# RWKV scan of a two-layer backbone: operands without zero halves, and a state tile apart from the values

## The chip, the cores and the metric

The kernel runs on one core of one Trainium2 chip. The metric is the device time of one execution in microseconds (us); several executions are timed, and one is profiled. The engines are named as the profile names them: PE is TensorE's matmul, PEld its weight load, DVE is VectorE, ACT is ScalarE, POOL is GpSimd, SP is SyncE, which issues the DMA transfers.

## The reference, cut to what matters

A backbone of two layers runs over 1024 latent and 256 context tokens. Each layer projects its input once for four groups of heads (mLSTM, Hyena, retention, RWKV-7), runs the groups, and mixes their outputs through one output projection; a feed-forward network follows. The RWKV group has four heads of 64 channels. For each head and direction it keeps a 64 x 64 state S and does for every token, in short:

```
S <- S diag(w_t) + (S a_t) b_t^T + v_t k_t^T
y_t = S r_t
```

The kernel does this in chunks of 64 tokens: within a chunk it forms the products of a, r with b, k (the tiles G), inverts a unit lower triangular 64 x 64 matrix for each head (the tile XT), and then updates the state once per chunk. All products are float32.

## The kernel before, in words

Each layer runs projections and retention first, and then the stretch of the scan: the generator `rwkv` for ten stages, woven into `mlstm` and `ada_steps` (the side work), and at last `load_wo` and the output projection. Stage s handles one tile of 128 tokens forward and one backward (index d), two chunks each (index c or ch), two feature halves (f) and in each an even and an odd head (q). Within iteration s the program is written in the order inverse of stage s+1, chain of stage s, tail of stage s+1, prep of stage s+2; the order of instructions on each engine is then set by the framework's scheduler from its own timing model, so that an edit at one place can move rows at others.

- `rwkv_prep` loads r, k, a (rkk), V into VSA and again into SV, multiplies W2 by TWA (L492, PSUM tile pbank), and makes AR (a and r scaled by decays; L524 and L525) and bk (b and k; L515, L526). AR has two halves of columns for each head parity, and in each the other parity's 64 rows are zero: they are cleared once, ahead of the scan (L450). The products bk x AR (L529) go to the PSUM tile dbank, and a masked copy of them is G (L530). Corners of G go to NB (L535, L536); bk is transposed through dbank (L540) into bt (L541).
- `rwkv_inverse` transposes NB into LM (L550) and runs 31 steps of two operations on POOL for one half and on DVE for the other (L557, L558): the longest string of small operations in a stage.
- `rwkv_tail` builds XT.
- `rwkv_chain` is the recurrence over chunks, twice per stage (i) and per direction. In one PSUM tile (cbank) it sums b0 = G x V + AR x state (L611, L612), copies it to U (L614), multiplies by XT (L615), copies the result to VSA (L617), sums b2 = identity x state + bt x VSA (L621, L622), and scales b2 into the next state in SV (L624). y is summed in ybank (L629, L630) and added into YF (L637). V stands in SV beside the state, in the other 64 rows, because L611 and L612 share a 128-row operand there.

PSUM tiles come from pools: cbank 2, ybank 1, pbank 1, dbank 2, mbank 2 (mbank is the side work's).

Of the kernel before, what the change touches and what calls it, by code (L numbers as in the profile page):

```python
# [10 lines left out]
F32=mybir.dt.float32  # L11
F32R=mybir.dt.float32r
BF16=mybir.dt.bfloat16
ACTF=mybir.ActivationFunctionType
# [415 lines left out]
def rwkv(K,l,pv,last,p1,p2,p3):  # L430
# [8 lines left out]
    TWA=p1.tile([128,2,2,128],F32,name="TWA"); nc.gpsimd.memset(TWA,0.0)  # L439
# [4 lines left out]
    for a in range(2):  # L444
        r=slice(64,128) if a==0 else slice(0,64); o=slice(0,64) if a==0 else slice(64,128)
# [3 lines left out]
    AR=[p1.tile([128,2,2,2,2,2,64],F32,name="AR%d"%i) for i in range(3)]  # L449
    for t in AR: nc.gpsimd.memset(t[64:128,:,:,:,0],0.0); nc.gpsimd.memset(t[0:64,:,:,:,1],0.0)  # L450
    XT=[p1.tile([128,2,4,128],F32,name="XT%d"%i) for i in range(2)]
# [18 lines left out]
def rwkv_prep(K,C,s):  # L470
# [3 lines left out]
    VSA,SV=[p.tile([128,2,2,2,2,64],F32,tag=n,name=n,bufs=2) for n in ("VSA","SV")]  # L474
    f,g=FWT[s],BWT[s]
    ALL=slice(0,2); PAIR=[(ALL,slice(f,g+1,g-f))] if f<g else [(0,f),(1,g)]
    for i in range(2):
        r=slice(i*64,i*64+64); tw=K.D['twa'][r].rearrange("p (n t) -> p n t",t=128)
        for o,n in PAIR: nc.sync.dma_start(C['TWA'][r,i,o],tw[:,n])
    for o,n in PAIR: nc.sync.dma_start(rkk[:,o],K.D['wrk'][:,n])  # L480
    for q in range(2):
        r=slice(64,128) if q==0 else slice(0,64)
        for X in (VSA,SV):
            for o,n in PAIR: nc.sync.dma_start(X[r,q,o].rearrange("p d c f e -> p d (c f e)") if o is ALL else X[r,q,o].rearrange("p c f e -> p (c f e)"),K.D['wv'][n,q].rearrange("n p c x -> p n (c x)") if o is ALL else K.D['wv'][n,q].rearrange("p c x -> p (c x)"))
    VSA,SV=[X.rearrange("p q d c f e -> p d c q f e") for X in (VSA,SV)]
# [27 lines left out]
    for a in range(2):  # L513
        for ft in range(2): act(out=bk[:,:,ft,:,a],in_=As[:,:,ft].rearrange("p d (c t) -> p d c t",t=64),func=ACTF.Identity,scale=C['kas'][:,a,0,ft:ft+1],bias=C['kas'][:,a,1,ft:ft+1])
        for d in range(2): tt(out=bk[:,d,:,:,a],in0=bk[:,d,:,:,a],in1=v4(rkk[:,d,4-2*a:6-2*a]),op=A.mult)  # L515
# [930 lines left out]
```

## Time and profile before

| | |
|---|---|
| time of three runs | median 4255.34 us (4251.47 to 4255.76) |
| profiled execution | 4269.9 us, its span 4268.0 us |
| mean granted TensorE clock | 0.94 of full |
| busy share of the span | PE 93%, PEld 75%, DVE 63%, ACT 33%, POOL 23% |
| scan of layer 0, first inverse's start to last one's end | about 806 to 1159 us |
| scan of layer 1 | about 2987 to 3353 us |

The shares are means over stages with different limits: most of the span is projections and feed-forward network, where PE streams without a break; the two scans are 719 us of 4268 together. In the rows below, "PE MATMUL" rows count each float32 product twice, since it runs as two passes. Behind the bar of a row of groups stands its busy time in us and the mean duration of one instruction in ns.

### The profile page before, as it was taken

The numbers are of one execution on the slowest core, as the hardware profiler recorded it, in microseconds if no ns is written. First come the engines' busy times: TensorE is split into PE (matmuls) and PEld (weight loads), VectorE is DVE, ScalarE is ACT, GpSimd is POOL, SyncE is SP. The second block draws the span as 40 slices with busy tenths as digits, with TensorE's granted clock in tenths as the row PEclk, the third lists the DMA queues.
The fourth block names the chain that finished last, engine by engine and source line by source line (L and its number), as shares of the span: only waits on it lengthen the run. The fifth ranks groups of instructions, "written<-read, shape, count | busy, mean of one in ns | idle before, by whom it ended". The sixth has DMA issues, their size and how long they took to land.

```text
span 4268.0 us, 65334 instructions
## 1 busy us (share of the span) xinstructions
PE 3956.8 (93%) x24976; PEld 3210.9 (75%) x24976; DVE 2672.2 (63%) x5412; ACT 1416.9 (33%) x2855; POOL 979.7 (23%) x2158
## 2 busy tenths in 40 slices
PE   5999999699979999999997999996899899999998
PEld 3878877566668888888884688885666678888886
DVE  5655665789769444444449555676888684444447
ACT  4433343554344211211123433344544342112121
POOL 3320023466512000000021221024666320000002
PEclk6999999789989999999998999997899699999999
DMA  4235444343343111111113235553332431111112
GB/s 166 74 102 177 149 153 122 112 143 116 122 160 119 45 40 34 41 40 35 37 35 124 82 91 154 169 162 114 122 115 84 136 114 55 48 41 55 45 50 99
DMA packets 477138, 414.16 MB, mean 97 GB/s; under 512 B 48827, under 2 KB 443284, under 8 KB 474010
## 3 DMA queue, kind: packets, MB, share of 16 engines
q1 hardware_dynamic: 476826, 409.99, 31.0%
q8 instruction: 197, 3.23, 0.3%
q14 instruction: 115, 0.94, 0.1%
HBM read 323.65 MB, written 86.25 MB: 96 GB/s over the span
## 4 chain that ended last, share of the span: by engine, by line
PE 52%; DVE 11%; DMA 3%; issue 2%; POOL 1%; ACT 1%; SPq 0%; ACTq 0%; DVEq 0%; POOLq 0%
PE bank L1022 9%; PE bank L1023 9%; PE bank L1024 9%; PE dbank L1022 6%; PE dbank L1023 6%; PE dbank L1024 6%; DVE bst L983 1%; DMA xt<-x 1%; DVE facc L1205 1%; PE bank L186 1%; PE bank L187 1%; DMA wst<-in_w_out 1%; PE dbank L529 0%; DVE facc L1206 0%; DVE facc L1274 0%
## 5 line engine op out<-in xcount | busy, mean ns | idle before, releaser
L1022 PE MATMUL dbank<-uh,wh 128*128 128x512 f32 (+1 forms) x2120 | 765.3, 370 | 8.8 <-ACT tmpB L398 5.7
L1023 PE MATMUL dbank<-ul,wh 128*128 128x512 f32 (+1 forms) x2120 | 761.2, 368 | 0.0
L1016 DVE TENSOR_TENSOR wl<-wst,wh 128x1024 fp32r<-128x1024 f32 x146 | 185.5, 1272 | 491.9 <-ACT wh L1015 367.3
L1024 PE MATMUL dbank<-uh,wl 128*128 128x512 f32 (+1 forms) x2120 | 480.6, 367 | 0.0
L1022 PEld LDWEIGHTS dbank<-uh,wh 128*128 128x128 f32 x2120 | 401.4, 189 | 85.0 <-ACT tmpB L398 6.1
L1023 PEld LDWEIGHTS dbank<-ul,wh 128*128 128x128 f32 x2120 | 401.6, 189 | 68.9 <-issue 1.1
L1024 PEld LDWEIGHTS dbank<-uh,wl 128*128 128x128 f32 x2120 | 365.9, 188 | 70.5 <-issue 1.5
L1264 DVE TENSOR_TENSOR facc<-facc,bank 128x512 f32<-128x512 f32 x324 | 221.8, 686 | 205.1 <-PE bank L1024 205.1
L1022 PE MATMUL bank<-uh,wh 128*128 128x512 f32 (+1 forms) x920 | 334.9, 372 | 4.5 <-ACT uh L1010 4.5
L1233 POOL MEMSET fz<- 128x1 f32 x132 | 7.2, 98 | 1433.6 <-DVE fc L1248 1433.6
L1023 PE MATMUL bank<-ul,wh 128*128 128x512 f32 (+1 forms) x920 | 335.1, 372 | 0.8 <-DVE ul L1011 0.8
L1022 PE MATMUL bank<-wdh,gh 128*128 128x512 f32 x792 | 314.9, 400 | 17.9 <-DVE facc L1278 8.7
L1023 PE MATMUL bank<-wdl,gh 128*128 128x512 f32 x792 | 310.5, 392 | 1.0 <-DVE wdl L1016 1.0
L1024 PE MATMUL bank<-wdh,gl 128*128 128x512 f32 x792 | 248.1, 392 | 0.0
L1015 ACT ACTIVATE wh<-wst 128x1024 fp32r<-128x1024 f32 x146 | 154.8, 1060 | 238.1 <-PE dbank L1023 168.4
L1015 ACT ACTIVATE wdh<-wst 128x1024 fp32r<-128x1024 f32 x46 | 48.8, 1062 | 529.4 <-PE bank L1024 427.7
L558 POOL TENSOR_TENSOR XL<-XL,lt 128x48 f32<-128x48 f32 (+26 forms) x620 | 204.4, 330 | 47.7
L557 POOL TENSOR_TENSOR lt<-LM,XL 128x48 f32<-128x48 f32 (+26 forms) x620 | 187.1, 302 | 119.4 <-ACT XL L551 45.0
L1024 PE MATMUL bank<-uh,wl 128*128 128x512 f32 (+1 forms) x920 | 211.9, 372 | 0.0
L1022 PEld LDWEIGHTS bank<-uh,wh 128*128 128x128 f32 x920 | 174.1, 190 | 36.1 <-ACT uh L1010 5.6
L1023 PEld LDWEIGHTS bank<-ul,wh 128*128 128x128 f32 x920 | 174.2, 189 | 31.9 <-DVE ul L1011 1.7
L1022 PEld LDWEIGHTS bank<-wdh,gh 128*128 128x128 f32 x792 | 149.7, 189 | 59.4 <-DVE facc L1278 14.9
(476 smaller groups left out, 8132.3 us busy)
## 6 DMA issues: line engine op xcount, KB each, us to landing
wst<-in_ffn_w_up SPq DMA_DIRECT2D x88, 512.0 KB
adaw<-in_ada_w SPq DMA_DIRECT2D x160, 256.0 KB
wst<-in_w_in SPq DMA_DIRECT2D x58, 512.0 KB
wst<-in_ffn_w_down SPq DMA_DIRECT2D x46, 512.0 KB
df<-in_c_F SPq DMA_DIRECT2D x10, 1344.0 KB
xt<-x SPq DMA_DIRECT2D x26, 512.0 KB
df<-in_c_I SPq DMA_DIRECT2D x8, 1344.0 KB
rkk<-wrk SPq DMA_DIRECT2D x10, 1024.0 KB
```

What stands on the lines that cost most here:

```text
L186: mm(dst_re,F[:,i],pre(slot),start=True,stop=False); mm(dst_re,F[:,i+1],pim(slot),start=False,stop=True)
L187: mm(dst_im,F[:,i],qim(slot),start=True,stop=False); mm(dst_im,F[:,i+2],qre(slot),start=False,stop=True)
L557: e.tensor_tensor(out=t_,in0=LM[:,j,j+1:32].unsqueeze(2).to_broadcast([128,n,m]),in1=X[h][:,j:j+1,0:m].to_broadcast([128,n,m]),op=A.mult)
L558: e.tensor_tensor(out=X[h][:,j+1:32,0:m],in0=X[h][:,j+1:32,0:m],in1=t_,op=A.add)
L983: for h in range(2): nc.vector.bn_stats(out=st[:,h],in_=x[h])
L1015: k.nc.scalar.activation(out=h,in_=st,func=ACTF.Copy)
L1016: k.nc.vector.tensor_tensor(out=lo,in0=st,in1=h,op=ALU.subtract)
L1022: mm(ps,lh,rh,start=(i==0),stop=False)
L1023: mm(ps,lh,rl,start=False,stop=False)
L1024: for i,((lh,ll),(rh,rl)) in enumerate(pairs): mm(ps,ll,rh,start=False,stop=(i==n-1 and more is None))
L1205: for o,i,gg in zip([y[:,h] for h in hs],x,[g[:,h] for h in hs]) if parts else [(y,x,g)]: stt(out=o,in0=i,scalar=m,in1=gg,op0=ALU.subtract ...
L1264: else: tt(out=d,in0=d,in1=ps,op=ALU.add)
```

## The change

AR loses its zero half: 64 columns of even heads stand in rows 0 to 63, those of odd heads in rows 64 to 127, and each DVE or POOL operation that fills it now covers 128 rows at once, so that one takes the place of two. TWA and XT are halved in the same way, and the memsets of AR and TWA go. Products that had 128 rows with a zero half become two products of 64 rows, one in each half of the array's rows: G has sixteen per stage in place of eight, those of a direction in two banks, one for each parity q, and the W2 products stand in the same way. pbank is gone: the W2 products take both dbanks, and ybank has two banks, one for each parity. SV, the second copy of V, is replaced by S, which holds the state alone; its load of V (two or four transfers in a stage's prep, 60 in all) goes, b2's identity product is one of 128 x 128 in place of four, and the next state is written by one DVE operation in place of two. In b0 and b1 all products are now 64 x 64; y has 128 x 64 products of G and 64 x 64 ones of AR.

```
-    AR=[p1.tile([128,2,2,2,2,2,64],F32,name="AR%d"%i) for i in range(3)]
-    for t in AR: nc.gpsimd.memset(t[64:128,:,:,:,0],0.0); nc.gpsimd.memset(t[0:64,:,:,:,1],0.0)
+    AR=[p1.tile([128,2,2,2,2,64],F32,name="AR%d"%i) for i in range(3)]
...
-    VSA,SV=[p.tile([128,2,2,2,2,64],F32,tag=n,name=n,bufs=2) for n in ("VSA","SV")]
+    VSA=p.tile([128,2,2,2,2,64],F32,tag="VSA",name="VSA",bufs=2)
+    S=p.tile([128,2,2,2,64],F32,tag="SV",name="S",bufs=2)
...
-    bb=[K.pbank(),K.pbank()]
-    for i in range(2):
-        for d in range(2):
-            for ft in range(2):
-                o=slice(d*256+ft*128,d*256+ft*128+128); mm(bb[i][:,o],C['W2'][:,o],C['TWA'][:,i,d],start=True,stop=True)
+    bb=[bank(),bank()]
+    for d in range(2):
+        for ft in range(2):
+            for i in range(2):
+                r=slice(i*64,i*64+64); o=slice(d*256+ft*128,d*256+ft*128+128); mm(bb[i][:,o],C['W2'][r,o],C['TWA'][r,d],start=True,stop=True)
...
-        for q in range(2):
-            r=slice(q*64,q*64+64)
-            (nc.gpsimd if d==0 else nc.vector).tensor_tensor(out=ar[r,d,:,:,q,0],in0=v4(rkk[r,d,6:8]),in1=Wp[r],op=A.mult)
-            tt(out=ar[r,d,:,:,q,1],in0=v4(rkk[r,d,0:2]),in1=W[r],op=A.mult)
+        (nc.gpsimd if d==0 else nc.vector).tensor_tensor(out=ar[:,d,:,:,0],in0=v4(rkk[:,d,6:8]),in1=Wp,op=A.mult)
+        tt(out=ar[:,d,:,:,1],in0=v4(rkk[:,d,0:2]),in1=W,op=A.mult)
...
-        for c in range(2):
-            b=bank()
-            for f in range(2): mm(b[:,f*256:f*256+256],bk[:,d,f,c].rearrange("p a t -> p (a t)"),ar[:,d,f,c].rearrange("p q a t -> p (q a t)"),start=True,stop=True)
+        b=[bank(),bank()]
+        for cf in range(4):
+            for q in range(2):
+                r=slice(q*64,q*64+64); c,f=cf//2,cf%2
+                mm(b[q][:,cf*128:cf*128+128],bk[r,d,f,c].rearrange("p a t -> p (a t)"),ar[r,d,f,c].rearrange("p a t -> p (a t)"),start=True,stop=True)
...
-                for r,q in HQ: mm(b0[r,f*64:f*64+64],G[64-q*64:128-q*64,d,ch,f,q,0:64],SV[64-q*64:128-q*64,d,ch,q,f],start=True,stop=False)
-                for r,q in HQ: mm(b0[r,f*64:f*64+64],ar[:,d,f,ch,q,0],SV[:,d,ch,q,f],start=False,stop=True)
+                for q in range(2): mm(b0[H[1-q],f*64:f*64+64],G[H[q],d,ch,f,q,0:64],VSA[H[q],d,ch,q,f],start=True,stop=False)
+                for q in range(2): mm(b0[H[1-q],f*64:f*64+64],ar[H[q],d,f,ch,0],S[H[q],d,ch,f],start=False,stop=True)
...
-                for f in range(2):
-                    for r,q in HQ: mm(b2[r,f*64:f*64+64],K.ident[:,r],SV[:,d,ch,q,f],start=True,stop=False)
-                    for r,q in HQ: mm(b2[r,f*64:f*64+64],bt[:,d,ch,f,q],VSA[:,d,ch,q,f],start=False,stop=True)
-                bv=b2.rearrange("p (f e) -> p f e",f=2); SN,cn=(SV,1-ch) if i==0 else (Pn['SV'],d)
-                for r,q in HQ: tt(out=SN[r,d,cn,q],in0=bv[r],in1=rho[r,i,d].unsqueeze(2).to_broadcast([64,2,64]),op=A.mult)
+                mm(b2,K.ident,S[:,d,ch].rearrange("p f e -> p (f e)"),start=True,stop=False)
+                for f in range(2):
+                    for q in range(2): mm(b2[H[q],f*64:f*64+64],bt[:,d,ch,f,q],VSA[:,d,ch,q,f],start=False,stop=f==1)
+                SN,cn=(S,1-ch) if i==0 else (Pn['S'],d)
+                tt(out=SN[:,d,cn],in0=b2.rearrange("p (f e) -> p f e",f=2),in1=rho[:,i,d].unsqueeze(2).to_broadcast([128,2,64]),op=A.mult)
...
-                    for d in range(2): mm(yo(q,d,f),ar[:,d,f,i^d,q,1],SV[:,d,i^d,q,f],start=False,stop=True)
+                for d in range(2):
+                    for q in range(2): mm(yo(q,d,f),ar[H[q],d,f,i^d,1],S[H[q],d,i^d,f],start=False,stop=True)
...
-        psum(k,cbank=2,ybank=1,pbank=1,dbank=2,mbank=2)
+        psum(k,cbank=2,ybank=2,dbank=2,mbank=2)
```

The scheduler makes its order anew, and two places on PE show what comes of it. The first is the prep of the first stages in layer 0, where PE works through the G products (L529), the transposes of bk (L540) and the next stage's W2 products (L492). Before, in PE's order:

```order
L529 MATMUL dbank_6817<-AR0_6743,bk_6799 128x256 x2
L529 MATMUL dbank_6821<-AR0_6743,bk_6799 128x256 x2
L492 MATMUL pbank_7034<-TWA_6727,W2_6721 128x128 x4
L540 MATMUL dbank_6829<-ident_72,bk_6799 128x128 x4
L529 MATMUL dbank_6841<-AR0_6743,bk_6799 128x256 x2
L492 MATMUL pbank_7436<-TWA_6727,W2_6721 128x128 x4
L529 MATMUL dbank_6845<-AR0_6743,bk_6799 128x256 x2
L540 MATMUL dbank_6853<-ident_72,bk_6799 128x128 x4
```

After, at the same place, where the lines have become L528 (G products), L539 (transposes) and L491 (W2 products); L711 and L717 are the mLSTM's. The first two rows are the last of four such pairs:

```order
L528 MATMUL dbank_6803<-AR0_6739,bk_6787 128x128
L528 MATMUL dbank_6804<-AR0_6739,bk_6787 128x128
L539 MATMUL dbank_6819<-ident_72,bk_6787 128x128 x4
L528 MATMUL dbank_6829<-AR0_6739,bk_6787 128x128 x4
L528 MATMUL dbank_6830<-AR0_6739,bk_6787 128x128 x4
L711 MATMUL mbank_7626<-me_7617,cmdec_7528 128x10 x4
L539 MATMUL dbank_6845<-ident_72,bk_6787 128x128 x4
L717 MATMUL mbank_7633<-cmsel_7529,mW_7612 128x12 x7
L491 MATMUL dbank_7021<-TWA_6724,W2_6718 128x128 x4
```

Two things moved. The G products of the forward direction alternate between two banks, that is between the two halves of the array's rows, while those of the backward direction come four and four, each four in one half. And the W2 products of the next stage, which stood between the G products and had a bank of their own, stand behind the last transpose.

The second place is the chain of a stage in the middle of layer 0's scan. Before, PE has the products of y (L629, L630) among those of b2 (L621, L622), and all four use 128 rows and 64 columns of the array:

```order
L621 MATMUL cbank_9438<-SV_7015,ident_72 64x64 x2
L622 MATMUL cbank_9438<-VSA_7014,bt_7073 64x64 x2
L629 MATMUL ybank_9346<-VSA_7014,G_7072 64x64
L630 MATMUL ybank_9346<-SV_7015,AR1_6744 64x64 x2
L629 MATMUL ybank_9346<-VSA_7014,G_7072 64x64 x2
L733 MATMUL mbank_8012<-ident_72,mk_8013 128x128 x2
```

After, the same products are L619 (identity, 128 x 128), L621 (bt), L628 (G, 128 x 64) and L630 (AR, 64 x 64); L739 and L973 are side work:

```order
L619 MATMUL cbank_9356<-S_7007,ident_72 128x128
L621 MATMUL cbank_9356<-VSA_7006,bt_7061 64x64 x4
L628 MATMUL ybank_9331<-VSA_7006,G_7060 64x64
L628 MATMUL ybank_9332<-VSA_7006,G_7060 64x64
L739 MATMUL mbank_7852<-mV_7526,kb_7847 64x65 x4
L973 MATMUL mbank_7859<-adaw_7817,sc_83 2x128 x4
L973 MATMUL mbank_7859<-adaw_7819,sc_83 2x128 x4
L630 MATMUL ybank_9331<-S_7007,AR1_6740 64x64
L630 MATMUL ybank_9332<-S_7007,AR1_6740 64x64
```

The shape of the array's use now changes between L619 and L621 and between L628 and L630, and no longer between the two lines of b0, which are both 64 x 64. Over the whole scan such changes between neighbours on PE, counted in the two orders, go from 511 to 598 in layer 0 and from 437 to 521 in layer 1; within them, the 117 and 120 between the lines of b0 go, and 126 and 120 come between L628 and L630 and between L619 and L621.

## Rows read from the trace of the kernel before

**Rows 1.** The page: busy time, share of the span and instructions of each engine
```profile
PE 3956.8 (93%) x24976; PEld 3210.9 (75%) x24976; DVE 2672.2 (63%) x5412; ACT 1416.9 (33%) x2855; POOL 979.7 (23%) x2158
```

**Rows 2.** Stretches: us, busy PE PEld DVE ACT POOL, clock, DMA share, GB/s
```profile
806.00:1159.00 353.00, 319.87 (x3811) 237.94 (x3812) 305.80 (x972) 159.78 (x461) 229.24 (x660) 0.88 0.40 124
2987.00:3353.00 366.00, 322.80 (x3642) 243.80 (x3641) 323.92 (x995) 165.87 (x481) 231.37 (x659) 0.85 0.35 110
```

**Rows 3.** Line L550 in each scan: min/median/max ns, first to last start
```profile
L550 DVE STREAM_TRANSPOSE LM<-NB x10: 1924/1952/1967, 804.5 to 1121.8; 128x1024 f32<-128x1024 f32 x10
...
L550 DVE STREAM_TRANSPOSE LM<-NB x10: 1929/1958/1992, 2984.9 to 3322.0; 128x1024 f32<-128x1024 f32 x10
```

**Rows 4.** Chain that ended last, 2951 to 3388 us: shares by line
```profile
by line: issue 8.2%; PE dbank L529 4.8%; DVE LM L550 3.8%; PE mbank L973 3.7%; DVE lt L557 3.7%; POOL lt L557 3.3%; DVE XL L558 3.3%; POOL XL L558 3.2%; PE pbank L492 2.6%; PE cbank L611 2.6%; DMA wst<-in_w_out 2.5%; PE cbank L612 2.4%; DVE
```

**Rows 5.** Groups by line and shape, 2951 to 3390 us (layer 1)
```profile
L524 POOL TENSOR_TENSOR AR<-rkk,Ep 64x256 f32<-64x256 f32 x20 | 14.3, 715 | 34.0 <-PE cbank L612 24.5 <-ACT Ep L506 8.7
L525 DVE TENSOR_TENSOR AR<-rkk,Ep 64x256 f32<-64x256 f32 x20 | 9.9, 496 | 0.6 <-DMA rkk<-wrk 0.3
L526 DVE TENSOR_TENSOR bk<-bk,Ep 128x256 f32<-128x256 f32 x20 | 9.4, 474 | 0.2
L624 DVE TENSOR_TENSOR SV<-cbank,rho 64x128 f32<-64x128 f32 x76 | 21.8, 287 | 11.2 <-PE cbank L622 9.8 <-PE cbank L612 0.6
L637 DVE TENSOR_TENSOR YF<-ybank,YF 128x128 f32<-128x128 f32 x16 | 3.5, 282 | 1.7 <-PE ybank L630 1.6
```

**Rows 6.** Timeline of PE in a chain: start, duration, line
```profile
1045.23 0.29 PE L622 MATMUL cbank<-VSA,bt 128*64 128x64 f32 x4
1045.35 0.29 PE L621 MATMUL cbank<-SV,ident 128*64 128x64 f32 x4
...
1046.64 0.34 PE L612 MATMUL cbank<-SV,AR 128*64 128x64 f32 x4
1046.90 0.33 PE L611 MATMUL cbank<-SV,G 64*64 64x64 f32 x4
1047.16 0.34 PE L612 MATMUL cbank<-SV,AR 128*64 128x64 f32 x4
```

**Rows 7.** Timeline of PE in retention, products of 64 rows (L846)
```profile
2938.24 0.71 PE L846 MATMUL bank<-rT 64*128 64x128 f32 x4
2938.88 0.43 PE L852 MATMUL bank<-rqkv,rS 128*128 128x64 f32 x2
...
2939.47 0.72 PE L846 MATMUL bank<-rT 64*128 64x128 f32 x8
2940.12 0.43 PE L852 MATMUL bank<-rqkv,rS 128*128 128x64 f32 x2
```

**Rows 8.** Timeline of PE in one stage's prep, layer 0
```profile
919.79 1.99 PE L529 MATMUL dbank<-AR,bk 128*128 128x256 f32 x8
922.46 1.16 PE L492 MATMUL pbank<-TWA,W 128*128 128x128 f32 x8
```

**Rows 9.** Lines L541, L536 and L550, 915 to 950 us: first and last start
```profile
L541 ACT ACTIVATE bt<-dbank x2: 597/597/597, 926.7 to 931.4; 128x512 f32<-128x512 f32 x2
...
L536 ACT ACTIVATE NB<-G x4: 292/306/310, 933.9 to 934.8; 32x128 f32<-32x128 f32 x4
...
L550 DVE STREAM_TRANSPOSE LM<-NB x1: 1948/1948/1948, 944.0 to 944.0; 128x1024 f32<-128x1024 f32 x1
```

**Rows 10.** Timeline of SP's queue at the start of layer 1's scan
```profile
2954.20 0.61 SPq L484 DMA_DIRECT2D SV<-wv  x1
...
2958.34 1.33 SPq L484 DMA_DIRECT2D SV<-wv  x2
```

**Rows 11.** Timeline of SP's queue at the end of layer 0's scan
```profile
1206.68 0.37 SPq L659 DMA_DIRECT2D yw<-gq  x1
...
1219.59 0.36 SPq L659 DMA_DIRECT2D ym<-gq  x1
```

**Rows 12.** Timeline of PE in layer 0's retention: idle before, and its releaser
```profile
723.14 0.69 PE L853 MATMUL bank<-rSS,rT 128*128 128x64 f32 x2 [2.10 <-POOL rSS L827]
```

More of the change, by code (lines that the diff above doesn't have):

```diff
@@ L444, in rwkv @@
     for a in range(2):
[L445 removed]
+        r=slice(a*64,a*64+64); o=slice(64-a*64,128-a*64)
         nc.gpsimd.memset(kas[o,a],-0.5)
@@ L448, in rwkv @@
         nc.vector.tensor_scalar(out=kas[r,a,1],in0=pv['ka'][r],scalar1=-0.5,scalar2=1.0,op0=ALU.mult,op1=ALU.add)
-    AR=[p1.tile([128,2,2,2,2,2,64],F32,name="AR%d"%i) for i in range(3)]
-    for t in AR: nc.gpsimd.memset(t[64:128,:,:,:,0],0.0); nc.gpsimd.memset(t[0:64,:,:,:,1],0.0)
-    XT=[p1.tile([128,2,4,128],F32,name="XT%d"%i) for i in range(2)]
+    AR=[p1.tile([128,2,2,2,2,64],F32,name="AR%d"%i) for i in range(3)]
+    XT=[p1.tile([128,2,4,64],F32,name="XT%d"%i) for i in range(2)]
     for t in XT: nc.gpsimd.memset(t,0.0)
@@ L514, in rwkv_prep @@
         for ft in range(2): act(out=bk[:,:,ft,:,a],in_=As[:,:,ft].rearrange("p d (c t) -> p d c t",t=64),func=ACTF.Identity,scale=C['kas'][:,a,0,ft:ft+1],bias=C['kas'][:,a,1,ft:ft+1])
-        for d in range(2): tt(out=bk[:,d,:,:,a],in0=bk[:,d,:,:,a],in1=v4(rkk[:,d,4-2*a:6-2*a]),op=A.mult)
+        for d in range(2): tt(out=bk[:,d,:,:,a],in0=bk[:,d,:,:,a],in1=v4(rkk[:,d,2+2*a:4+2*a]),op=A.mult)
     G=p.tile([128,2,2,2,2,128],F32,tag="G",name="G",bufs=3); bt=p.tile([128,2,2,2,2,64],F32,tag="BKT",name="bt",bufs=3)
@@ L541, in rwkv_prep @@
         act(out=bt[:,d].rearrange("p c f q e -> p (c f q e)"),in_=b,func=ACTF.Copy)
-    return dict(VSA=VSA,SV=SV,io=io,ar=ar,G=G,bt=bt,NB=NB,XT=C['XT'][s%2])
+    return dict(VSA=VSA,S=S,io=io,ar=ar,G=G,bt=bt,NB=NB,XT=C['XT'][s%2])
 def rwkv_inverse(K,C,P):
@@ L576, in rwkv_tail @@
             lo=slice(q*64,q*64+32); hi=slice(q*64+32,q*64+64)
-            mm(b[hi,o],G[lo,0,c,f,q,32:64],T2[lo,:,:,0,u],start=True,stop=True)
-            mm(b[lo,o],G[hi,1,c,f,q,0:32],AX[hi,u],start=True,stop=True)
+            mm(b[hi,o],G[lo,0,c,f,1-q,32:64],T2[lo,:,:,0,u],start=True,stop=True)
+            mm(b[lo,o],G[hi,1,c,f,1-q,0:32],AX[hi,u],start=True,stop=True)
     act(out=Q.rearrange("p u t -> p (u t)"),in_=b[:,0:128],func=ACTF.Copy)
@@ L584, in rwkv_tail @@
             lo=slice(q*64,q*64+32); hi=slice(q*64+32,q*64+64)
-            mm(b[lo,o],Q[hi,u],XT[hi,0,u,hi],start=True,stop=True)
-            mm(b[hi,o],Q[lo,u],XT[lo,1,u,lo],start=True,stop=True)
+            mm(b[lo,o],Q[hi,u],XT[hi,0,u,32:64],start=True,stop=True)
+            mm(b[hi,o],Q[lo,u],XT[lo,1,u,0:32],start=True,stop=True)
     bv=b[:,0:128].rearrange("p (u t) -> p u t",t=32)
@@ L589, in rwkv_tail @@
         lo=slice(q*64,q*64+32); hi=slice(q*64+32,q*64+64)
-        act(out=XT[lo,0,:,hi],in_=bv[lo],func=ACTF.Copy)
-        nc.vector.tensor_copy(out=XT[hi,1,:,lo],in_=bv[hi])
+        act(out=XT[lo,0,:,32:64],in_=bv[lo],func=ACTF.Copy)
+        nc.vector.tensor_copy(out=XT[hi,1,:,0:32],in_=bv[hi])
 def rwkv_chain(K,C,P,Pn,s):
     nc=K.nc; act=nc.scalar.activation; tt=nc.vector.tensor_tensor; mm=nc.tensor.matmul; A=ALU
-    p=C['p']; tiles=(FWT[s],BWT[s]); G,XT,bt,ar,VSA,SV,io=(P[n] for n in ('G','XT','bt','ar','VSA','SV','io'))
-    HQ=((slice(0,64),0),(slice(64,128),1))
+    p=C['p']; tiles=(FWT[s],BWT[s]); G,XT,bt,ar,VSA,S,io=(P[n] for n in ('G','XT','bt','ar','VSA','S','io'))
+    H=(slice(0,64),slice(64,128))
     rho=p.tile([128,2,2,2],F32,tag="rho",name="rho",bufs=2)
@@ L602, in rwkv_chain @@
     need_y=not(C['last'] and s<2); YF=C['YF']
-    if need_y: y=K.ybank(); yb=[y[:,0:256],y[:,256:512]]
+    if need_y: yb=[K.ybank(),K.ybank()]
     for i in range(2):
@@ L613, in rwkv_chain @@
             U=p.tile([128,2,64],F32,tag="U%d"%d,name="U")
             act(out=U.rearrange("p h t -> p (h t)"),in_=b0,func=ACTF.Copy)
-            for f in range(2): mm(b1[:,f*64:f*64+64],XT[:,d,ch*2+f],U[:,f],start=True,stop=True)
+            for f in range(2):
+                for r in H: mm(b1[r,f*64:f*64+64],XT[r,d,ch*2+f],U[r,f],start=True,stop=True)
             bv=b1.rearrange("p (f e) -> p f e",f=2)
-            act(out=VSA[0:64,d,ch,0],in_=bv[0:64],func=ACTF.Copy); nc.vector.tensor_copy(out=VSA[64:128,d,ch,1],in_=bv[64:128])
+            act(out=VSA[0:64,d,ch,1],in_=bv[0:64],func=ACTF.Copy); nc.vector.tensor_copy(out=VSA[64:128,d,ch,0],in_=bv[64:128])
```

20 lines of the change are left out of this document (9 added, 11 removed).

## The prediction

> **What bounds the kernel now.** I read the page first, then the stretches of the two scans, the chain of waits inside them, and last single lines and the timeline. On the page PE is busy for 93% of the span [rows 1], but that is a mean over long stages of projections which this change does not touch. What it touches lies in the two scans. There DVE is busy for 306 of 353 us in layer 0 (87%) and 324 of 366 us in layer 1 (89%), PE for 320 and 323, POOL for 229 and 231 [rows 2]. [...] The transposes that open the ten inverses start 317.3 us apart from first to last in layer 0, and 337.2 us in layer 1 [rows 3]: nine steps of 35.3 and 37.5 us. Everything in a stage must fit into that step.
>
> The chain of waits of layer 1's scan belongs to no engine alone: "issue", PE's G products (L529), the transposes to LM, the side work (L973) and the inverse on DVE and POOL follow one another with 2 to 5% each [rows 4]. Where the chain changes engines so often, taking time from one engine shortens the stretch by a part of what is taken. This is the main choice of the sum below.
>
> **DVE.** An AR operation on 64 rows lasts 496 ns; one of the same 256 columns on 128 rows lasts 474 ns (L525 and L526) [rows 5]. So joining two into one halves the cost. Sixty of the old kind per layer on DVE (three groups of twenty like that of L525) become thirty: 60 x 0.475 = 28.5 us, of which 14.2 go. A new state on 64 rows lasts 287 ns, on 128 rows 282 (L637, of the same 128 columns) [rows 5]: 76 become 38, and 10.9 us go. DVE loses 25.1 us per layer, 7.7% of its busy time. The bounds are 0 (all of it lay beside other work) and 25.1. I take half, 12.5 us: DVE is almost full, yet the chain is on PE, POOL and issue for the other part. POOL's twenty AR operations of 715 ns become ten of about the same length and save 7 us per layer; I count 0 for it beyond DVE's half, since POOL idles for a third of the stretch [rows 2].
>
> **PE.** Four items.
>
> First, b0. Neighbours of one shape start 0.12 us apart for a block of four records (1045.23 to 1045.35), while the blocks of L611 and L612, which differ in the rows of the array that they use, start 0.26 us apart (1046.64, 1046.90, 1047.16) [rows 6]. So a change of shape costs about 0.14 us. b0's four blocks cost 1.05 us, and with one shape about 0.5: 55% less. L611 and L612 have 2.6 and 2.4% of the chain's 437 us [rows 4], 22 us; 55% of it is 12 us.
>
> Second, G. In retention four records of 64-row products take 0.64 us (2938.24 to 2938.88), where they do not alternate between the row halves, and eight that alternate take 0.65 us [rows 7]. Alternating, two run in the time of one. Sixteen G products of 128 columns hold as many columns as eight of 256 did, so they cost the same without pairing and half with it. In the changed order the forward direction alternates and the backward one does not, so a quarter of L529 goes: 4.8% of 437 is 21 us [rows 4], and a quarter is 5. Bounds 0 and 10.
>
> [...]
>
> Third, W2's products: eight of twenty groups alternate in the new order, so a fifth of 2.6% of 437 us [rows 4]: 2 us.
>
> Fourth, the new changes of shape. The two orders have 87 and 84 more changes than before, after b0's 117 and 120 are taken off; about 204 per layer are new. At 0.14 us that is 29 us of PE per layer. More than half of them are within y and the new state (126 and 120); y's lines do not show among the listed lines of the chain [rows 4], and its result is wanted only by YF. I take 9 us, the third that PE has of the chain's listed shares (L529, L973, L492, L611 and L612 come to 16 of the 44% listed), a little less because y is in none of them. Bounds 0 and 29. b2's and y's shorter products I leave at 0 for the same reason.
>
> PE's sum is -12 -5 -2 +9 = -10 us per layer.
>
> **SP and the rest.** At the start of layer 1's scan SP issues the SV loads between those of VSA and the stage's other tiles, in four groups: twice 0.61 us and twice about 1.3 [rows 10]. They go: 3.9 us at most, and 1.5 taken, since the first stage's rkk stands ahead of them. In layer 0, PE waits 2.10 us in retention for POOL's rSS [rows 12], which stands behind the AR memsets; they go, so I take 2 us once.
>
> **The sum.** Layer 1: -12.5 -10 -1.5 = -24. In layer 0 the scan's last store is issued at 1206.68 but the mLSTM's at 1219.59 [rows 11], so 13 us pass after the scan has ended. The side work shares the engines and moves too, but not by all of it: I take half, -12, and -2 for the memsets. Together -38. The profiled execution took 4269.9 us, 0.3% over the median of the runs, 4255.3; the difference is applied to the median: **4217 us**.
>
> **The rivals.** (B) Nothing measurable. If the string of inverses on POOL alone sets the step, halving DVE's work only makes DVE wait. For it: L557 and L558 stand on the chain for both engines with 3.2 to 3.7% each [rows 4]. Against it: POOL is busy for two thirds only [rows 2]. Then the start, the memsets and what little AR costs ahead of the inverse remain: 4250 us.
>
> (C) The changes of shape eat the gain. If all 29 us per layer count instead of 9, layer 1 loses 20 and layer 0 half of that: 4217 + 30 = 4247 us. For it: PE is busy for nine tenths of both scans [rows 2].
>
> [...]
>
> (E) Slower: dbank becomes the bound. Before, W2's products of the next stage ran at 922.46 us, on a bank of their own, in the middle of the G products that started at 919.79 [rows 8]. In the changed order they stand behind the last transpose of bk, and both dbanks must be free: the copy of the last one starts at 931.4 us and takes 0.6 [rows 9], so they start at 932.0, 9.5 us later. Behind them in PE's order wait the side work's L717 and the chain of the stage, for which U (L614) and the new state wait in turn. The whole prep of the next stage hangs on them, and so the next LM. What is there to spare is the time from the last NB copy's end (934.8 + 0.3) to the transpose that reads it at 944.0 [rows 9]: 8.9 us here. Where it is 6 us in another stage, 3.5 are lost. Over nine steps that is +31 us in layer 1, and in layer 0 +31 less the 13 that the mLSTM covers: 4217 + 49 = 4266 us. It decides where the delay is over the spare time by more than the 2.5 us per stage that the rest saves. Against it: G's products of a stage come after W2's anyway, and the second W2 bank waited before for pbank to be read.
>
> **How the numbers follow.** The sum as it stands, with its own range 4190 to 4241: 0.52. Its lower end has DVE whole and G whole (12.6 + 5 more in layer 1, half of that in layer 0), its upper end DVE at a quarter and half of the further changes of shape (6 + 10, and half of that). B has 0.14, C 0.16, E 0.18. A change under 0.2% (8.5 us) can't be told from none. Faster than 4246.8 are nearly all of the first, two fifths of C and a quarter of B: 0.61. Slower than 4263.8 is most of E and a tail of the others: 0.18. The rest, 0.21, is no change. The range of 8 in 10 goes from 4176, half as far again beyond the lower end for what the shorter products of b2 and y may give, to 4268, which takes in E's price.
>
> **What would show it.** Right: DVE's busy time in each scan falls by about 25 us, the steps between LM transposes fall to about 33 and 35 us, L609 and L610 blocks start 0.12 us apart, the forward G blocks run in half the time. Wrong: LM steps unchanged with DVE idling before the inverse (B); PE's busy share as before or higher, with gaps at each L628 to L630 (C); L491 late by about 10 us, waiting for the bt copy, and the idle of DVE or POOL ended by LM or G (E). The number fails as a whole if the scheduler's new order moves side work into the places that became free.

## The result, and the profile after

The changed kernel is slower: median 4310.99 us of four runs (4290.81 to 4319.80) against 4255.55 for the kernel before on the same chip, a ratio of 1.0123 with a 95% interval of 1.0085 to 1.0161. The forecast was 4217. The profiled execution, at 4319.8 us, is the slowest of the four; its span is 50.0 us longer than that of before.

The page's first line, which answers to [rows 1]:

```profile
PE 4001.0 (93%) x25160; PEld 3237.5 (75%) x25160; DVE 2629.3 (61%) x5276; ACT 1419.3 (33%) x2857; POOL 959.8 (22%) x2120
```

DVE has 42.9 us less in both layers together (50.2 were forecast), PE 44.2 us more.

The LM transposes of both scans of the changed kernel, the answer to [rows 3]:

```profile
L549 DVE STREAM_TRANSPOSE LM<-NB x10: 1920/1934/1964, 824.7 to 1205.5; 128x1024 f32<-128x1024 f32 x10
...
L549 DVE STREAM_TRANSPOSE LM<-NB x10: 1916/1948/1977, 3041.8 to 3372.9; 128x1024 f32<-128x1024 f32 x10
```

Layer 0's nine steps take 380.8 us in place of 317.3, 42.3 each; layer 1's 331.1 in place of 337.1, 36.8 each. The first transpose of layer 0 comes 20.2 us later than before. From layer 0's last transpose to layer 1's first it is 1836.3 us, before it was 1863.1: a part of the side work that followed the scan now runs inside it, for the last store of layer 0's group norms comes 74.2 us after the last transpose (1279.7), before 97.8 us (1219.6). So 20.2 + 63.5 - 26.8 - 6.0, and -0.9 behind, make the 50.0. The loss is all in layer 0 and ahead of its scan; layer 1 gained 6 of the 24 us that were forecast for it.

Three stretches of the changed kernel, with the columns of [rows 2]: the end of layer 0's retention and the start of its scan, then the two scans from the first inverse to the last one's end; the last row is the first stretch in the kernel before:

```profile
740.00:800.00 60.00, 50.62 (x278) 44.12 (x278) 16.36 (x40) 19.20 (x41) 11.27 (x20) 0.55 0.19 63
826.00:1239.00 413.00, 369.83 (x4083) 266.30 (x4083) 309.69 (x947) 172.65 (x486) 229.28 (x653) 0.79 0.33 104
3043.00:3403.00 360.00, 322.03 (x3784) 239.62 (x3782) 306.82 (x945) 172.03 (x493) 228.87 (x651) 0.84 0.33 103
...
740.00:800.00 60.00, 41.24 (x327) 35.27 (x325) 39.00 (x75) 31.06 (x69) 15.38 (x26) 0.85 0.46 127
```

DVE is down to 75% and 85% of the scans, from 87% and 89%. PE is busy for as large a share as before, but its granted clock in layer 0's scan is 0.79, which was 0.88 [rows 2], and 0.55 in the first stretch, where the kernel before had 0.85 for the same 60 us.

PE's timeline in a chain and in two preps of the changed kernel (start, duration, line), the answer to [rows 6] and [rows 8]:

```profile
947.15 0.28 PE L610 MATMUL cbank<-S,AR 64*64 64x64 f32 x4
947.26 0.28 PE L609 MATMUL cbank<-VSA,G 64*64 64x64 f32 x4
947.38 0.28 PE L610 MATMUL cbank<-S,AR 64*64 64x64 f32 x4
...
1007.55 0.33 PE L630 MATMUL ybank<-S,AR 64*64 64x64 f32 x4
1007.82 0.34 PE L628 MATMUL ybank<-VSA,G 128*64 128x64 f32 x4
1008.08 0.33 PE L630 MATMUL ybank<-S,AR 64*64 64x64 f32 x4
...
1009.44 1.16 PE L528 MATMUL dbank<-AR,bk 64*128 64x128 f32 x16 [0.66 <-POOL lt L556]
1014.64 1.16 PE L528 MATMUL dbank<-AR,bk 64*128 64x128 f32 x8
1017.85 1.16 PE L528 MATMUL dbank<-AR,bk 64*128 64x128 f32 x8
```

b0's blocks start 0.115 us apart (0.26 before), y's, whose shapes now differ, 0.265 apart. Sixteen records of the forward G, which alternate between the row halves, take 1.16 us, and of the backward one, which do not, eight take 1.16; before, a direction took 1.99 [rows 8].

So in this stage the forward direction got faster, 1.16 us for 1.99, and the backward one slower, two blocks of 1.16 for 1.99. PE's whole busy time on G in layer 1's scan, before and after:

```profile
L529 PE MATMUL dbank<-AR,bk 128*128 128x256 f32 x160 | 50.4, 450 | 3.2 <-DVE G L530 2.2 <-DVE AR L525 0.9
L528 PE MATMUL dbank<-AR,bk 64*128 64x128 f32 x320 | 46.0, 341 | 6.2 <-DVE bk L523 5.3 <-POOL lt L556 0.6
```

It fell by 9%, not by the quarter of the forecast; in layer 0 it fell from 48.5 to 48.0 us.

DVE and POOL in layer 1's scan by line and shape, the answer to [rows 5]:

```profile
L623 DVE TENSOR_TENSOR S<-cbank,rho 128x128 f32<-128x128 f32 x38 | 10.8, 285 | 12.4 <-PE cbank L621 11.9
L521 POOL TENSOR_TENSOR AR<-rkk,Ep 128x256 f32<-128x256 f32 x10 | 8.1, 806 | 5.4 <-ACT Ep L505 5.4
L522 DVE TENSOR_TENSOR AR<-rkk,En 128x256 f32<-128x256 f32 x10 | 4.9, 486 | 0.1
```

The new state costs 10.8 us in place of 21.8, an AR operation on 128 rows 486 ns. These halved as forecast.

What did not hold is the order of a stage. W2's products, the transpose that reads their stage's result, and the copy before them, in layer 0's last step (min/median/max ns, first to last start; the timeline's row gives the copy of bt):

```profile
L491 PE MATMUL dbank<-TWA,W x16: 272/272/373, 1162.8 to 1171.1; 64*128 64x128 f32 x16
...
L549 DVE STREAM_TRANSPOSE LM<-NB x2: 1932/1943/1954, 1162.6 to 1205.5; 128x1024 f32<-128x1024 f32 x2
```

```profile
1160.27 0.58 ACT L540 ACTIVATE bt<-dbank 128x512 f32<-128x512 f32 x1
```

The last copy of bt ends at 1160.85, W2's products start 2 us later, and the LM transpose of their own stage starts at 1205.5, 42.7 us after them. Read in this way over all steps but each layer's first stage, W2's first product stands 28 to 53 us ahead of its LM transpose; before it stood 59 to 131 ahead. Against steps of about 37 to 42 us the prep now runs about one step ahead of its use; before it ran about two to three and a half ahead.

### The profile page after: what moved, and what is told of

Its sections match the earlier page's. It is cut to its first block, busy times and chain, and to the rows that moved or that the text cites. A ratio compares the mean times of both kernels' runs of the same rounds, so it can differ in the third digit from the quotient of the medians.

```text
span 4318.0 us, 65299 instructions
## 1 busy us (share of the span) xinstructions
PE 4001.0 (93%) x25160; PEld 3237.5 (75%) x25160; DVE 2629.3 (61%) x5276; ACT 1419.3 (33%) x2857; POOL 959.8 (22%) x2120
```

## The experiments

Ratios are to the kernel before on the same chip, with 95% intervals. "Clock" is the granted clock from the first to the last LM transpose of each layer. Where medians of different kernels are subtracted, they can come from different chips; the kernel before took 4258.7 to 4262.2 us on them. Each build gets a new order from the scheduler, which no run here separates from its edit. The code shown for an edit is cut to the lines that tell it from the others.

**What to tell apart.** Theory 1: the loss is PE at its lower clock (0.79 in layer 0's scan, 0.88 before), which the products of 64 rows bring. Theory 2: it is the wait for dbank, the rival of the prediction. Four kernels first.

The first puts back the memsets, and with them PE's order in layer 0's retention:

```
-    AR=[p1.tile([128,2,2,2,2,64],F32,name="AR%d"%i) for i in range(3)]
+    AR=[p1.tile([128,2,2,2,2,64],F32,name="AR%d"%i) for i in range(3)]; [nc.gpsimd.memset(t[r],0.0) for t in AR for r in (slice(64,128),slice(0,64))]
```

> The changed kernel with POOL memsets of the old number and size on AR, and one on TWA, put back ahead of the scan (they do nothing for the result now). With them PE's order in layer 0's retention is again that of the kernel before, row for row. Theory 1 (clock: the loss is PE at its lower granted level, and the 20 us that are lost before the first inverse of layer 0 come from the new order in retention alone): the first LM transpose of layer 0 is back at about 805 us (825 in the changed kernel), and the time at 4270 to 4292. Theory 2 (banks: the loss is in the scan, because the W2 and G products wait for dbank): the steps of layer 0's scan stay at 42 us, and no more than the 20 us come back, 4290 or more.

The median is 4315.87 us, ratio 1.0134 (1.0117 to 1.0151). The LM transposes of layer 0 in this kernel:

```profile
L549 DVE STREAM_TRANSPOSE LM<-NB x10: 1907/1940/1967, 807.6 to 1156.0; 128x1024 f32<-128x1024 f32 x10
```

The first one is back at 807.6, so the 17 us ahead of the scan did come from the order in retention, where no product had changed. But the time did not follow: layer 0's steps take 348.4 us in place of 380.8, and layer 1's 353.9 in place of 331.1. Neither theory had that: theory 1 expected a shorter time, theory 2 steps of 42 us in layer 0. The start of layer 0 is not what the 55 us hang on. With the same products, the memsets and the order that they brought took 32 us from one scan and put 23 on the other.

The second undoes the prep, with its memsets, 64-row AR operations and 128-row products:

```
-                mm(b[q][:,cf*128:cf*128+128],bk[r,d,f,c].rearrange("p a t -> p (a t)"),ar[r,d,f,c].rearrange("p a t -> p (a t)"),start=True,stop=True)
+            for f in range(2): mm(b[:,f*256:f*256+256],bk[:,d,f,c].rearrange("p a t -> p (a t)"),ar[:,d,f,c].rearrange("p q a t -> p (q a t)"),start=True,stop=True)
```

> The changed kernel with the prep of before: AR and TWA with zero halves and their memsets, AR operations of 64 rows, G products of 128 rows and 256 columns, W2 products of 128 rows; both still in dbank, and the state tile, b0, b1, b2 and y as changed. Theory 1 (the products of 64 rows let the granted clock fall): granted clock of both scans back at 0.85 or more, time 4225 to 4260. Theory 2 (banks: W2's products in both dbanks are the fault): these are kept, so 4290 or more.

4277.30 us, 1.0053 (1.0030 to 1.0075); the clocks are 0.87 and 0.91. Three fifths of the loss are gone and the clock is back; the time lies between the two theories, above 4260 and below 4290.

The third makes G's and W2's products of 64 rows, both in dbank, in the kernel before; the state stays in SV:

```
-            for f in range(2): mm(b[:,f*256:f*256+256],bk[:,d,f,c].rearrange("p a t -> p (a t)"),ar[:,d,f,c].rearrange("p q a t -> p (q a t)"),start=True,stop=True)
+                mm(b[q][:,cf*128:cf*128+128],bk[r,d,f,c].rearrange("p a t -> p (a t)"),ar[r,d,f,c,q].rearrange("p a t -> p (a t)"),start=True,stop=True)
```

> The kernel before with one part of the change: G and W2 products of 64 rows in two banks (dbank; ybank 2, no pbank), all else as before, AR and TWA still padded and SV still there. Theory 1: granted clock of the scans falls to 0.80 or less and the time is 4280 or more. Theory 2: likewise slow, 4280 or more, but with the clock as before and the W2 products waiting for the copies out of dbank. If it is at 4255, the loss belongs to the other part, the state tile and the 64 x 64 products of the chain.

4343.99 us, 1.0201 (1.0186 to 1.0217), clocks 0.79 and 0.78. Both theories expected 4280 or more, but only theory 1 the lower clock. This part alone costs more than the whole change.

The fourth adds dense products to the changed kernel, in the ring that W2's products are in:

```
-    bb=[bank(),bank()]
+    bb=[bank(),bank()]; [mm(bb[0],K.ident,C['W2'],start=True,stop=True) for _ in range(4)]
```

> The changed kernel with four float32 products of 128 rows and 512 columns ahead of each stage's W2 products, into the same bank, overwritten by them: 80 in all, about 69 us of PE at the higher clock by the same form elsewhere in the program, which do nothing for the result. Theory 1 (clock): the granted clock of the scans rises to 0.85 or more, and the time falls in spite of the added work, to 4260 to 4300. Theory 2 (banks): dbank is held longer in each stage and the time rises by 50 us or more, over 4360.

4350.05 us, 1.0216 (1.0186 to 1.0246), clocks 0.83 and 0.87: the clock rose in layer 0 (0.77 before the edit) and the time rose too, by 39 us for some 69 us of work (the estimate of the expectation). Neither expectation is met; it decides nothing by itself.

**Banks and rows taken apart.** The changed kernel with pbank for W2, and for that 128-row products of AR in y:

```
-    bb=[bank(),bank()]
+    bb=[K.pbank(),K.pbank()]
...
-        psum(k,cbank=2,ybank=2,dbank=2,mbank=2)
+        psum(k,cbank=2,ybank=1,pbank=1,dbank=2,mbank=2)
```

> The changed kernel with a bank of its own for the W2 products again (pbank 1, taken one group after the other, each of 64 rows; ybank 1). For that, y's products of AR are of 128 rows again: AR holds a once and r with zero halves, so DVE's r operations are of 64 rows as before. All else as changed. Theory 2 (banks: in the changed kernel W2's products run 28 to 53 us ahead of the LM transpose that needs them, before 80 to 130, because they wait for both dbanks): they run 70 us or more ahead again, the steps of the scans fall to 33 to 37 us, time 4200 to 4245. Theory 1 (products of 64 rows let the granted clock fall): the clock of both scans stays at 0.8 and the time at 4290 or more.

4294.88 us, 1.0082 (1.0067 to 1.0097). W2's products stand 59 to 123 us ahead again, so that prediction of theory 2 holds, and the clocks stay at 0.77 and 0.81, as theory 1 said. The time falls by 16 us only, to theory 1's range, 50 us above theory 2's.

The state tile alone, with prep and banks as before:

```
-    VSA,SV=[p.tile([128,2,2,2,2,64],F32,tag=n,name=n,bufs=2) for n in ("VSA","SV")]
+    VSA=p.tile([128,2,2,2,2,64],F32,tag="VSA",name="VSA",bufs=2)
+    S=p.tile([128,2,2,2,64],F32,tag="SV",name="S",bufs=2)
```

> The state tile alone: prep, banks and AR as in the kernel before, with the state in S, V from VSA, b0 and b1 of 64 x 64, one identity product, one operation for the next state, no second load of V. Both theories: no slower than before, 4220 to 4250, since DVE has 11 us less in each scan and b0 fewer changes of shape. If it is slower than 4270, a part of the loss belongs to the state tile itself.

4252.37 us, 0.9977 (0.9965 to 0.9989), just above the expected range, and faster than before by about the least that can be told. Clocks 0.88 and 0.87.

Only W2's bank, in the kernel before:

```
-    bb=[K.pbank(),K.pbank()]
+    bb=[bank(),bank()]
```

> The kernel before with one edit: the W2 products take the two dbanks and not pbank (ybank 2 in its place). No product changes its shape. Theory 2: W2's products fall back to 30 to 50 us ahead of their LM transpose, the steps grow to 38 us or more, time 4280 to 4330. Theory 1: no change of rows, so no change, 4245 to 4265.

4295.60 us, 1.0075 (1.0056 to 1.0095). W2's products stand 32 to 51 us ahead. Here is the rival of the prediction by itself. The two scans of this kernel, first to last LM transpose:

```profile
809.00:1135.70 326.70, 284.76 (x3399) 212.64 (x3399) 290.36 (x890) 152.26 (x452) 203.58 (x590) 0.88 0.38 115
3017.40:3354.00 336.60, 297.46 (x3315) 220.52 (x3315) 298.75 (x904) 155.65 (x455) 211.82 (x594) 0.86 0.33 102
```

The clock is that of before, 0.89 and 0.86 between the same points, so this loss is not the clock's. Theory 2 has the time right, but not the steps, which it put at 38 us or more: they take 36.3 us in layer 0 (35.3 before) and 37.4 in layer 1, as before. The loss lies for the most part in layer 0: from the first transpose to the last store of its group norms it is 433.2 us, before 415.1.

Rows of 64 without W2's bank: W2's products and G's as in the third kernel, W2's on pbank:

```
-                o=slice(d*256+ft*128,d*256+ft*128+128); mm(bb[i][:,o],C['W2'][:,o],C['TWA'][:,i,d],start=True,stop=True)
+                r=slice(i*64,i*64+64); o=slice(d*256+ft*128,d*256+ft*128+128); mm(bb[i][:,o],C['W2'][r,o],C['TWA'][r,i,d],start=True,stop=True)
```

> The kernel before with G and W2 products of 64 rows, as in the second experiment of this kind, but W2's on pbank as before: only G's two banks per direction and the rows change. Theory 2 (it is W2's bank): 4235 to 4270, against 4344 with W2 in dbank. Theory 1 (it is the 64 rows): the clock falls as there and the time is 4310 or more. In between, the two banks that each direction's G holds at once have a part of their own.

4346.21 us, 1.0205 (1.0188 to 1.0222), W2's products 60 to 147 us ahead. Its scans between the same points:

```profile
808.50:1157.80 349.30, 314.68 (x3525) 235.52 (x3524) 281.36 (x871) 148.44 (x435) 206.62 (x594) 0.77 0.35 108
3039.80:3392.10 352.30, 319.66 (x3537) 240.62 (x3539) 295.89 (x903) 154.75 (x445) 207.53 (x597) 0.80 0.33 104
```

The prep has all its lead and the loss is as large as with W2 in dbank; the clock is 0.77 and 0.80. Two edits remain in it besides G's rows: G's two banks per direction, and W2's rows. The next two kernels add them one by one with G at 128 rows:

```
-                mm(b[q][:,cf*128:cf*128+128],bk[r,d,f,c].rearrange("p a t -> p (a t)"),ar[r,d,f,c,q].rearrange("p a t -> p (a t)"),start=True,stop=True)
+                mm(b[q][:,cf*128:cf*128+128],bk[:,d,f,c].rearrange("p a t -> p (a t)"),ar[:,d,f,c,q].rearrange("p a t -> p (a t)"),start=True,stop=True)
```

> The kernel before with the changed kernel's two banks for each direction's G products, one for each parity, but each product still of 128 rows with the zero half of AR (16 of 128 columns in place of 8 of 256). W2 as before. If the loss of the kernel with G and W2 of 64 rows (4346 us) comes from the rows, as theory 1 says: granted clock of the scans at 0.86 to 0.90, time 4250 to 4275. If it comes from the two banks that are held at once (theory 2): 4310 or more, whatever the clock.

> The kernel before with G in two banks per direction of 128 rows, as in the first run of this call, and W2's products of 64 rows, on pbank, one group after the other so that no two of them run beside each other. Theory 1: W2's products have much to spare and are few (40 of the scan's products per stage and layer are others), so the clock loses little and the time is that of the first run of this call within 15 us. If the W2 products bring the low clock, 4310 or more.

Two banks with W2 as before: 4275.86 us, 1.0030 (1.0010 to 1.0050), clocks 0.92 and 0.85. W2's products of 64 rows too, by the edit shown last before this one: 4280.94, 1.0056 (1.0035 to 1.0076), clocks 0.87 and 0.87. So of the 84 us between the kernel before and the one with 64 rows (4261.65 to 4346.21), the two banks, with sixteen products for eight, cost about 14, W2's rows 5, which the intervals can't tell from none, and G's rows 65.

From the first LM transpose to the last store of layer 0's group norms, where each kernel has done the same work, these are the stretches of the kernel before, of the changed one, of the one with 128-row G (last above) and of the one with 64-row G, in this order:

```profile
804.50:1219.60 415.10, 376.20 (x4437) 280.29 (x4437) 345.41 (x1080) 183.34 (x505) 238.95 (x669) 0.89 0.38 120
```

```profile
824.70:1279.70 455.00, 405.37 (x4523) 293.66 (x4523) 339.21 (x1022) 188.28 (x520) 233.73 (x658) 0.80 0.32 102
```

```profile
808.70:1234.70 426.00, 384.75 (x4580) 291.81 (x4578) 351.31 (x1080) 183.96 (x505) 243.62 (x671) 0.88 0.38 117
```

```profile
808.50:1276.00 467.50, 416.98 (x4580) 307.89 (x4578) 352.68 (x1080) 186.78 (x507) 241.44 (x671) 0.79 0.35 106
```

Busy time times clock is 335, 324, 339 and 329 us: by this estimate PE has less to do with 64 rows, and it is busy for longer (405.37 us for 376.20, 416.98 for 384.75). From the third row to the fourth the stretch grows by 41.5 us, and 32.2 of them are busy time of PE.

**Is the clock the cause, or does it only go along?** The kernel with 64 rows got dense products in W2's pbank, where there is time to spare, in all stages:

```
-    bb=[K.pbank(),K.pbank()]
+    bb=[K.pbank(),K.pbank()]; [mm(bb[0],K.ident,C['W2'],start=True,stop=True) for _ in range(4)]
```

> The kernel before with G and W2 products of 64 rows, W2's on pbank (4346 us), and ahead of each stage's W2 products four float32 products of 128 rows and 512 columns into the same pbank, overwritten by them, 80 in all and some 69 us of PE. W2's products run 60 us or more ahead of their need there, so this work is not in the ring. Theory 1: the clock rises to 0.85 or more and the time falls by 20 us or more, to 4326 or less, in spite of the work. Theory 2: more work on a PE that is nine tenths busy, 4360 or more.

4337.30 us, 1.0200 (1.0165 to 1.0235), clocks 0.86 and 0.87. The clock came back as theory 1 said, but the time fell by 9 us and not by 20, and the intervals can't tell that from none; the added work, some 69 us of PE by the estimate, cost no time and gained none. That is in between the two theories. So the same was done in the first four stages alone (`range(6 if s<4 else 0)`), on the state tile, on the kernel with 64 rows and on the kernel before.

> The state tile alone (4252 us, prep and banks of before), and ahead of the W2 products of the first four stages of each layer six products of 128 rows and 512 columns into pbank, 48 in all, which do nothing for the result. Theory 1: the clock of the first steps, 0.6 to 0.8 there, rises to 0.85 or more, and the time falls under that of the state tile alone, 4225 to 4248. If the first steps do not hang on PE's clock: 4252 or more.

> The kernel before with G and W2 products of 64 rows, W2's on pbank (4346 us), and six products of 128 rows and 512 columns into pbank ahead of the W2 products of each layer's first four stages, 48 in all, some 41 us of PE at the higher clock, the most of it before and in the first step of the scans. Theory 1 (clock): the clock of the first three steps, 0.5 to 0.68 there, is 0.8 or more and the time falls to 4270 to 4330. If the 64-row products cost by their own time or order: 4346 or more.

> Control: the kernel before with the same 48 products added in the same place. Theory 1: its first steps have a clock of 0.65 to 0.9 already, so little comes back, and the time is 4240 to 4270. If the added products helped by something other than the clock of a slow start, both kernels would gain the same.

On the state tile: 4244.64 us, 0.9973 (0.9957 to 0.9990), clocks 0.92 and 0.89, no difference from the state tile alone (0.9977) that the intervals can tell. With 64 rows: 4303.32, 1.0101 (1.0077 to 1.0125), 43 us less than without them and in theory 1's range; the first three steps of layer 0 have a clock of 0.62, 0.62 and 0.71, before 0.50, 0.50 and 0.68, so less than expected. On the kernel before: 4298.53, 1.0078 (1.0058 to 1.0099), 36 us more, 29 above the expected range. The scans of these two between the LM transposes, 64 rows first:

```profile
819.40:1152.40 333.00, 307.89 (x3589) 229.50 (x3590) 280.34 (x867) 147.68 (x435) 202.91 (x592) 0.84 0.37 115
3024.90:3368.80 343.90, 309.11 (x3389) 228.10 (x3388) 288.36 (x885) 150.86 (x439) 210.35 (x594) 0.83 0.33 101
```

```profile
808.80:1126.70 317.90, 288.91 (x3402) 212.89 (x3402) 278.68 (x867) 143.32 (x429) 204.29 (x591) 0.88 0.38 118
3022.90:3346.00 323.10, 291.82 (x3251) 217.24 (x3251) 283.45 (x878) 149.38 (x434) 210.14 (x595) 0.89 0.35 107
```

The same useless work costs the one kernel 36 us and gives the other 43. Where it gives, it raises a low clock (0.77 and 0.80 to 0.84 and 0.83), and the scans get 16.3 and 8.4 us shorter. That speaks for the clock as cause. It is not a clean cross: the 36 us do not lie between the transposes (317.9 and 323.1 us for 317.3 and 337.1), but for the most part from layer 0's last transpose to layer 1's first (1896.2 us for 1863.1), and the profiled execution with 64 rows, the slowest of its four, shows 22 of the 43.

Then the pairing was taken away and the 64 rows kept:

```
-        for cf in range(4):
-            for q in range(2):
+        for q in range(2):
+            for cf in range(4):
```

> The kernel with G and W2 of 64 rows (4346 us), G's products with the parity in the outer loop, so that none stands beside one of the other half of the array's rows. Theory 1 (clock, by rows in use at a time): the clock is as low or lower, 0.75 to 0.80, and the time 4346 or more. If pairing is what keeps the clock low (less work for PE): the clock rises to 0.85 and the time falls under 4320.

4299.90 us, 1.0101 (1.0068 to 1.0133), clocks 0.82 and 0.82. By busy time times clock PE has more to do (394.83 us at 0.85 from the first transpose to the last store of layer 0's group norms, 336 us for 329), and the kernel is 46 us faster than with pairs (1.0205). So 46 of the 65 us of G's rows belong to the pairs, to their order or to what the scheduler made of them, and not to the 64 rows as such; what the pairs save on PE went with a lower clock (0.77 and 0.80). The same edit on the changed kernel, and on the changed kernel with pbank:

> The changed kernel with the parity in the outer loop of G's products, so that none stands beside one of the other half of the rows. If pairing lowers the clock and with it the speed of the scan (4346 to 4300 us on the kernel before): the clock of layer 0's scan rises from 0.77 to 0.82 or more and the time falls from 4311 to 4260 to 4290. If that gain belonged to the order that the scheduler happened to make: 4295 to 4325, no different from the changed kernel.

> The same edit on the changed kernel with a bank of its own for W2 (4295 us). If pairing and bank cost apart from each other: 4240 to 4270, near the state tile alone. If the gain of the last run belonged to its order alone: 4280 to 4310.

The changed kernel stays where it was: 4318.73 us, 1.0129 (1.0102 to 1.0157), clocks 0.79 and 0.78, which is what was expected if the gain of the last run belonged to its order. With pbank, where the same reading expected 4280 to 4310, it falls to 4245.44 us, 0.9967 (0.9951 to 0.9983), clocks 0.84 and 0.84:

```profile
811.80:1133.50 321.70, 286.24 (x3529) 215.20 (x3529) 266.30 (x840) 146.57 (x435) 203.18 (x584) 0.84 0.37 114
2988.90:3298.30 309.40, 275.82 (x3286) 208.20 (x3284) 268.41 (x832) 146.06 (x429) 202.77 (x586) 0.84 0.36 111
```

All versions side by side, as ratios to the kernel before:

| G's products | W2 on pbank | W2 in dbank |
|---|---|---|
| state in SV: 128 rows | 1 | 1.0075 |
| state in SV: 64 rows, pairs | 1.0205 | 1.0201 |
| state in SV: 64 rows, one parity after the other | 1.0101 | not run |
| state tile: 128 rows | 0.9977 | 1.0053 |
| state tile: 64 rows, pairs | 1.0082 | 1.0123 (the change) |
| state tile: 64 rows, one parity after the other | 0.9967 | 1.0129 |

"Pairs" are products that alternate between the row halves. W2's products are of 64 rows wherever G's are, and G has two banks for each direction there; with the state tile y's products of AR are of 64 rows in the dbank column and of 128 in the other. The edits don't add: W2's bank costs 0.8% with 128 rows, 0.4% or nothing with pairs, and the lack of pairs gives back 1% only where W2 has its bank. Three versions are about 0.3% faster than the kernel before, and their intervals can't tell them from one another: the state tile alone, the same with dense products in four stages, and the changed kernel with W2 on pbank and G's products unpaired.

## Why the prediction was wrong, by its own steps

**DVE** was right in kind and size (42.9 us in both layers for 50.2). What it is worth shows in the state tile alone: 9 us of the median (4261.65 to 4252.37), with 11 of 25 us per layer taken from DVE and b0 rid of its changes of shape. The sum had counted half of DVE's saving and 12 us for b0; by that rule the state tile was worth some 17 us in layer 1 and half as much in layer 0, 26 together. It was too much by far even where nothing else went wrong.

**The step that failed is G, the second item of PE.** It was given 5 us of gain per layer with bounds 0 and 10, and no loss: pairs cost PE half, and sixteen products without pairs were to cost the same as eight of twice the columns, so the time could only fall. The second premise failed already in the stage shown: two unpaired blocks take 2.32 us for 1.99, as two blocks of W2's eight records of 128 columns in [rows 8] would. G's busy time fell by 9% in layer 1 and by 1% in layer 0, not by a quarter. And the time rose: G's 64 rows cost 65 us in the kernel with the same banks, and what went along in nearly every such kernel is PE's granted clock. Without added products it is 0.85 to 0.92 in all twelve scans with 128-row G, and 0.77 to 0.84 in fifteen of the sixteen with 64-row G; the other one is layer 1 of the changed kernel at 0.86, where the scan lost nothing. [rows 2] shows 0.88 and 0.85 for the kernel before, and the sum let the clock stand as a constant. In these kernels it went with what PE was given.

**Rival E was the second cause, with its delay right and its chance too small.** W2's products do stand behind the last transpose, and start 2 us after its copy. The delay was put at 9.5 us against 8.9 to spare, from one stage; in fact the lead over the LM transpose falls from between 59 and 131 us to between 28 and 53, and by itself W2's bank costs 34 us on the kernel before (4261.65 to 4295.60) and 25 on the state tile (4252.37 to 4277.30). It was given 0.18, at 31 us in layer 1 and 18 in layer 0. By the profiles it is paid in layer 0: from the first transpose to the last store of the group norms 433.2 us for 415.1, and 432.8 for 406.4 on the state tile, while layer 1's steps take 336.6 for 337.1 and 318.6 for 323.8. So a loss in every step, as the rival had it, is not shown; why layer 0 alone pays stays open.

Put on one after the other, state tile, W2's bank, then the rest of the prep, the ratios go 0.9977, 1.0053, 1.0123: -0.2%, +0.8% and +0.7%. The last two come to some 60 us that the sum did not have; the rest of the way from 4217 to 4311 is for the most part gain that it had and that did not come.

The new changes of shape cost what the blocks of y show, 0.15 us each, but no run took them alone; the state tile alone has those of b2 and comes out faster. The start of layer 1 and the memsets were small either way; the memsets' removal gave the retention another order and cost 17 us ahead of layer 0's scan, where 2 were to be gained, and putting them back did not lower the time.

**What stays open.** That the low clock is the cause of G's loss is supported by the crossed pair (+36 and -43 us for the same added work), by the unpaired products and by PE's longer busy time for less work (by the estimate above), and not shown beyond doubt: the added products in all stages brought the clock back and the time by 9 us at most, and the unpaired G left the changed kernel where it was while W2 was in dbank. Step by step the two don't go together either: with 64 rows and W2 on pbank layer 0's first two steps have the lowest clock, 0.50, and take 35.0 and 28.0 us (34.6 and 38.2 before, at 0.63 and 0.82); it is the third that takes 57.2, at 0.68. How much of each difference is the scheduler's new order was not taken apart; it can't be held fixed under these edits. Packing the rows so that neighbours alternate in one direction only was not varied further.

## What to carry to other kernels

Before work is taken from a PE that is nearly full, look at its granted clock in that stretch: here, at 0.88, a saving of work for PE went with a clock of 0.79 and the time rose, so test such an edit alone and read the clock beside the time. Add up the busy time of the whole group as well: the forward products of one stage took 58%, the group 91% in layer 1. Removing zero padding by splitting products into row halves also took PSUM banks here; look at who held those banks, and how far ahead of its use that work ran. Where parts of a change are separable, as the state tile was here, build each by itself before the sum.

## What was not expected of the hardware

For 40 us of layer 0's scan in the changed kernel PE was recorded as busy without a break at a granted clock of 0.50. Two stretches of the changed kernel, one after the other, and the second of them in the kernel before:

```profile
960.00:980.00 20.00, 20.00 (x166) 14.70 (x166) 7.90 (x25) 5.64 (x20) 1.68 (x8) 0.50 0.20 64
980.00:1000.00 20.00, 20.00 (x195) 14.38 (x193) 8.46 (x28) 7.56 (x24) 4.97 (x17) 0.50 0.28 85
...
980.00:1000.00 20.00, 20.00 (x232) 13.25 (x221) 17.19 (x63) 8.18 (x26) 15.32 (x43) 0.91 0.55 173
```

PE has no idle time in these 40 us, and its clock is granted at 0.50 throughout. For the most part its work there is the 64-row G and W2 products, the chain's products, y's among them, and the side work's small ones. In the kernel before, the stretch from 980 to 1000 us was as full and had 0.91. So the profile's busy time is not what tells the two apart. What does, no run here shows.
